# A decoder step on one core: which engine issues the weight loads, the window copies and the stores of new rows

## The chip, the cores and the metric

The kernel runs on one core of one Trainium2 chip. A core has five engines with a queue each: TensorE (PE; its weight loads are listed as PEld), VectorE (DVE), ScalarE (ACT), GpSimd (POOL) and SyncE (SP). Each works through its own list in order and waits on semaphores where it needs another's result. A DMA is an entry of such a list: the engine waits for the conditions of the transfer, issues it, and goes on; the bytes are then moved by 16 DMA engines that all queues share. The metric is the time of one execution in microseconds (us) on the device.

## The reference

One layer of a hybrid decoder, for 256 prompt tokens and for 8 samples of 4 new tokens each over 2048 cached positions. Cut to what is computed:

```python
h = rms_norm(x, norm_g)
c_h, c_b, c_c, c_g, q, n_g, b_g, kv6, m_q, m_g = split_cols(h @ w_in)   # 2048 x 6680
y_a = silu(c_g) * short_conv(c_h, c_b, c_c)                             # group A
o_cmp, o_sel = nsa_cmp_sel(q, rope(q), pos, k_cmp, v_cmp, k_sel, v_sel) # group B, paged cache
o_win = window_attention(rope(q), win_k, win_v)
y_b = silu(n_g) * (g0 * o_cmp + g1 * o_sel + g2 * o_win)
y_m = silu(m_g) * gqa_attend(m_q, mem_k, mem_v)                         # group M, 256 memory tokens
y = rms_norm(x + concat(y_a, y_b, y_m) @ w_out, final_g)
```

`k_cmp` and `v_cmp` are weighted sums over blocks of 64 cached rows, so the whole paged cache is read. Beside `y` the step returns the new K and V rows (`o_kv` in the kernel), the memory K and V of the prompt (`o_mem`), the state of the convolution (`o_conv`), and the window buffers, whose old rows are copied from one place in HBM to another (`o_wk`, `o_wv`).

## The kernel before

**Weights.** All projections are made of 152 weight halves of 128 x 1024 float32 (512 KB): 16 of `w_mem`, 104 of `w_in`, 32 of `w_out`. Half `s` is loaded into `w{s}` (`w_load`, L169; five buffers, tag `wr`), rounded by ACT into `wh` (L179) and subtracted by DVE into `wl` (L184); PE then runs 24 matmuls over it (`product_half`, L198), 16 with `wh` and 8 with `wl`. Inside the matmuls of half `s` the program writes `wh` of half `s+2`, `wl` of half `s+1` and, at matmul 21, the load of half `s+6`. That load may start when `wl` of half `s+1` is done, since it takes that half's buffer. The first four halves are used as they are.

**Cache tiles.** Everything cached comes through six buffers `st` of 128 x 1024 float32 (tag `st`), in the order of a table of due times (`stages`, L644): pages of `ckc` (two DMAs a tile), of `ckk` and `ckv` (four DMAs a tile, `load_pages`, L277, with the page's number read by SP from `ptt` first), and plain tiles of `wk`, `wv`, `mk`, `mv`. A `ckc` tile is multiplied in place, its K half by DVE and its V half by POOL (`cmp_use`, L288; the multiply is L294 on both engines), POOL's half after DVE's, and summed by DVE one tile later (L316). The others go straight into matmuls of PE (`sk` and `od` for pages, `smd` and `omd` for the memory). A new load is issued when a tile is used up (`load_next`, L657).

**What sets the order.** The order on each engine is that of the program text: `chunk` (L114), called after every 12 matmuls, advances the side work by one step. So the loads of weights and of cache tiles stand interleaved in one list, SP's. ACT issues 13 stores: 12 of `o_kv` (L966, L971) and one of `o_conv` (L1059). POOL issues five stores of `o_mem` (L782, L784), beside its 64 multiplies. The 16 window copies (`window_copies`, L625) are issued by SP.

**Completion counters.** A listing of the program's order with its waits shows that the DMAs of SP and ACT together take eight counters in turn (`DMAHW0` to `DMAHW7`), and that each waits for the landing of the one that took the same counter before it, eight DMAs earlier. The DMAs of POOL have eight counters of their own (`DMASW0` to `DMASW7`).

Of the kernel before, what the change touches and what calls it, by code (L numbers as in the profile page):

```python
# [71 lines left out]
def decode_step(ctx, tc, xT, xN, memT, cst, w_in, w_mem, w_out, w_bg, pt, ckc, ckk, ckv, wk, wv, mk, mv,  # L72
# [96 lines left out]
    def w_load(s):  # L169
        if s < NH:  # L170
            raws[s] = pw.tile([128, 1024], F32, name=f"w{s}", tag="wr", bufs=WR)
            if s:
                nc.sync.dma_start(raws[s], wsrc[s])
            loading(DMA_PIECE)

    def w_hi(s):
# [448 lines left out]
    def window_copies():  # L625

        n = 0
        for hf in range(2):
            for rq in range(4):
                for out, in_ in ((o_wk[2 * hf + rq // 2, rq % 2], wk[2 * hf + rq // 2, rq % 2]), (o_wv[hf, rq], wv[hf, rq])):  # L630
                    while now[0] < min(T_WIN[0] + n * T_WIN[1], LAST_PASS):
                        yield 1
                    nc.sync.dma_start(out, in_)
                    n += 1
                    if now[0] >= LAST_PASS:
                        yield T_LAST
# [318 lines left out]
    def kv_tile(part, g, z):  # L955
        if part in (2, 4):
            i = part - 2 + g
            nc.scalar.activation(kk[:, i, :], z, AF.Copy)
            rope_in(i, z)
            if i == 3:  # L960
                yield 1
                yield from rope_out(lambda i, r: nc.scalar.activation(kk[0:32, i, :], r, AF.Copy))
                env["k"] = True
                yield 1
                for i in range(4):
                    nc.scalar.dma_start(o_kv[4 + (i // 2) * 4 + i % 2], kk[:, i, :])  # L966
            return
        dst = zt("A", "kv")
        nc.scalar.activation(dst, z, AF.Copy)
        yield 2  # L970
        nc.scalar.dma_start(o_kv[2 * part + g], dst)  # L971
        if part in (0, 1):
            t = zt("B", "pp")[:, :256].rearrange("p (n j) -> p n j", j=64)
            nc.vector.tensor_tensor(t, dst[:, :256].rearrange("p (n j) -> p n j", j=64),
                                    acmp[:, part].unsqueeze(1).to_broadcast([128, 4, 64]), op=ALU.mult)
            nc.vector.tensor_reduce(pool_p[:, part, g, :], t, axis=AX.X, op=ALU.add)
        if part in (3, 5):
            t = ptr.tile([128, 512], F32, name=f"vtp{part}{g}", tag="t")
            for s in range(2):
                transpose(t[:, s * 128:(s + 1) * 128], dst[:, s * 128:(s + 1) * 128], ident)  # L980
            if part == 3:
                transpose(t[0:64, 256:384], dst[:, 224:288], ident)
            else:
                transpose(t[0:32, 256:384], dst[:, 256:288], ident)
            nc.scalar.activation(vnat[part][:, :, g, :], t[:, :256].rearrange("p (s d) -> p s d", s=2), AF.Copy)
            o = 32 if part == 3 else 0
            nc.scalar.activation(Vn[o:o + 32, g, :], t[o:o + 32, 256:384], AF.Copy)
            env["v", part, g] = True
# [36 lines left out]
    def conv_tile(i, j, z):  # L1025
# [26 lines left out]
        elif j == 2:  # L1052
            nc.vector.tensor_tensor(ct["y"], ct["y"], z, op=ALU.mult)
        else:
            sg = silu2(z)
            yield 1
            nc.vector.scalar_tensor_tensor(mixed[:, i, :], ct["y"], 0.5, sg, op0=ALU.mult, op1=ALU.mult)
            if i == 3:
                nc.scalar.dma_start(o_conv, convo.rearrange("p i t -> p (i t)"))  # L1059
        return  # L1060
        yield

# [408 lines left out]
```

## Time and profile before

| | us |
|---|---|
| median of 3 runs | 649.82 |
| lowest and highest | 647.42, 649.86 |
| the profiled execution, its own time | 649.14 |
| its span, first instruction to last | 647.3 |

The profile lists for each engine the time in which it was busy. Rows of a window give, after the window and its length, each engine's busy time with the number of instructions, then the granted share of the TensorE clock, the mean busy share of the 16 DMA engines, and GB/s. Rows of waits give who waited for whom: total us, times, longest us. Rows of the timeline give start, duration, engine, line, operation, tiles, and in brackets the idle time of the engine before it with what ended it; `SPq` and `ACTq` are those engines' queues, in which DMAs are issued. Names stand without buffer numbers.

### The profile page before, as it was taken

How to read it: one execution, taken by the hardware profiler on the slowest of the kernel's cores; microseconds unless marked ns; L12 is line 12 of the kernel's file. 1: busy time of each engine (PE TensorE's matmuls, PEld its weight loads, DVE VectorE, ACT ScalarE, POOL GpSimd, SP SyncE). 2: the span in 40 equal slices, each digit the busy share in tenths (PEclk: the TensorE clock that was granted, in tenths of full speed). 3: DMA queues.
4: the chain of work that ended last, by engine and by line, in shares of the span. 5: the costliest groups of instructions: out<-in, count | busy, mean ns of one | idle time of the engine just before them, and what ended most of it. 6: DMA issues, size and time to landing. Idle time of an engine off the chain costs nothing.

```text
span 647.3 us, 13704 instructions
## 1 busy us (share of the span) xinstructions
PE 620.8 (96%) x4899; PEld 557.9 (86%) x4899; DVE 453.3 (70%) x721; ACT 290.2 (45%) x517; POOL 81.2 (13%) x79
## 2 busy tenths in 40 slices
PE   9999999999999999999999999999999999999992
PEld 7899999999997898887889787877888889999992
DVE  4788799988675676978669688774764544456754
ACT  4765545435553333543345333443343444445650
POOL 0002333222121210022112121200000000000000
PEclk9999999999999999999999999999999999999996
DMA  8999799989978989977889999898997898488824
GB/s 305 371 420 386 233 316 320 320 287 336 310 265 265 318 310 378 384 256 258 246 270 298 287 303 296 270 304 290 411 363 237 267 274 286 162 273 280 266 76 147
DMA packets 90726, 188.42 MB, mean 291 GB/s; under 512 B 10465, under 2 KB 47202, under 8 KB 90274
## 3 DMA queue, kind: packets, MB, share of 16 engines
q1 hardware_dynamic: 87072, 183.42, 83.5%
q10 hardware_dynamic: 3250, 3.07, 1.4%
q0 software_dynamic: 336, 1.05, 0.4%
q8 instruction: 39, 0.64, 0.4%
q14 instruction: 29, 0.24, 0.1%
HBM read 182.29 MB, written 13.60 MB: 303 GB/s over the span
## 4 chain that ended last, share of the span: by engine, by line
PE 65%; DMA 15%; DVE 12%; issue 3%; SPq 3%; ACT 2%; DVEq 0%; ACTq 0%
PE z L101 51%; DMA st<-ckc 4%; PE od L101 3%; DMA w<-w_in 3%; DVE pooled L316 3%; DMA st<-ckk 2%; DVE wl L184 2%; PE acc L101 2%; PE sk L101 2%; DMA o_kv<-kv 2%; SPq L280 2%; DVE st L294 2%; PE s L101 2%; DMA w<-w_mem 1%; DMA st<-mk 1%
## 5 line engine op out<-in xcount | busy, mean ns | idle before, releaser
L101 PE MATMUL z<-x,wh 128*128 128x288 f32 x1664 | 258.9, 303 | 0.0
L101 PEld LDWEIGHTS z<-x,wh 128*128 128x128 f32 x1664 | 230.0, 188 | 14.6 <-issue 13.0
L184 DVE TENSOR_TENSOR wl<-w,wh 128x1024 fp32r<-128x1024 f32 x148 | 183.5, 1240 | 31.8 <-PE z L101 19.2
L179 ACT ACTIVATE wh<-w 128x1024 fp32r<-128x1024 f32 x148 | 155.0, 1052 | 43.5 <-DMA w<-w_in 28.5
L101 PE MATMUL z<-x,wl 128*128 128x288 f32 x832 | 127.1, 295 | 2.5 <-DVE wl L184 2.3
L101 PEld LDWEIGHTS z<-x,wl 128*128 128x128 f32 x832 | 115.7, 188 | 3.6 <-DVE wl L184 3.6
L294 POOL TENSOR_TENSOR st<-st,cst 128x512 f32<-128x512 f32 x64 | 75.7, 1184 | 299.1 <-DVE st L294 142.6
L316 DVE TENSOR_REDUCE pooled<-st 128x16 f32<-128x1024 f32 x64 | 77.4, 1209 | 2.0 <-POOL st L294 2.0
L294 DVE TENSOR_TENSOR st<-st,cst 128x512 f32<-128x512 f32 x64 | 43.8, 685 | 9.5 <-DMA st<-ckc 8.9
L101 PE MATMUL z<-y,wh 128*128 128x288 f32 x256 | 37.0, 297 | 0.0
L101 PE MATMUL z<-y1a,wh 128*128 128x288 f32 x224 | 35.5, 298 | 0.0
L101 PEld LDWEIGHTS z<-y,wh 128*128 128x128 f32 x256 | 35.1, 188 | 0.0
L101 PEld LDWEIGHTS z<-y1a,wh 128*128 128x128 f32 x224 | 31.6, 188 | 1.6 <-issue 1.6
L1005 DVE SCALAR_TENSOR_TENSOR se<-se,z 128x288 f32<-128x288 f32 x16 | 7.2, 452 | 33.3 <-ACT se L1004 33.3
L101 PE MATMUL sk<-st,qz 128*32 128x256 f32 x320 | 25.8, 385 | 2.7 <-DMA st<-ckk 2.4
L101 PE MATMUL z<-m,wh 128*128 128x256 f32 x192 | 27.0, 286 | 0.7 <-ACT wh L179 0.7
L101 PEld LDWEIGHTS z<-m,wh 128*128 128x128 f32 x192 | 24.6, 191 | 1.4 <-ACT wh L179 0.9
L1164 DVE TENSOR_TENSOR P<-s,cst 128x512 f32<-128x512 f32 x12 | 8.3, 690 | 22.0 <-PE s L101 22.0
L1171 ACT ACTIVATE P<-P,nm 128x128 f32<-128x128 f32 (+1 forms) x32 | 14.2, 445 | 18.2 <-DVE nm L1168 18.2
L378 ACT ACTIVATE S<-sk 128x256 f32<-128x256 f32 x20 | 7.6, 382 | 31.9 <-PE sk L101 31.9
L101 PE MATMUL od<-st,PT 128*32 128x256 f32 x320 | 21.4, 385 | 0.0
L1004 ACT ACTIVATE se<-z 128x288 f32<-128x288 f32 x16 | 6.5, 406 | 31.2 <-PE z L101 31.2
(277 smaller groups left out, 623.6 us busy)
## 6 DMA issues: line engine op xcount, KB each, us to landing
w<-w_in SPq DMA_DIRECT2D x104, 512.0 KB, 6.2
st<-ckc SPq DMA_DIRECT2D x128, 256.0 KB, 5.2
st<-ckk SPq DMA_DIRECT2D x128, 128.0 KB, 4.5
st<-ckv SPq DMA_DIRECT2D x128, 128.0 KB, 3.6
w<-w_out SPq DMA_DIRECT2D x32, 512.0 KB, 5.1
w<-w_mem SPq DMA_DIRECT2D x15, 512.0 KB, 9.1
o_wk<-wk SPq DMA_DIRECT2D x8, 512.0 KB, 6.9
o_wv<-wv SPq DMA_DIRECT2D x8, 512.0 KB, 6.3
```

Of the source, the lines that this page charges most:

```text
L101: nc.tensor.matmul(out, a, b, **kw)
L179: nc.scalar.activation(his[s], raws[s], AF.Copy)
L184: (eng or nc.vector).tensor_tensor(los[s], raws.pop(s), his[s].bitcast(F32), op=ALU.subtract)
L280: nc.sync.dma_start(t[:, i * w:(i + 1) * w], src[ds(v, 1)].rearrange("a p c -> p (a c)"))
L294: done.append(eng.tensor_tensor(tm[:, :, kv], tm[:, :, kv], acmp[:, kv].unsqueeze(1).unsqueeze(1).to_broadcast([128, 2, 4, 64]), op=ALU.mu ...
L316: nc.vector.tensor_reduce(pv.rearrange("p a (c n) -> p c a n", n=2), t.rearrange("p (c a n j) -> p c a n j", c=2, a=4, j=64), axis=AX.X, o ...
L378: nc.scalar.activation(env["S", hf][:, o:o + 256], s[:, :256], AF.Copy)
L1004: nc.scalar.activation(e, z, AF.Tanh, scale=0.5)
L1005: nc.vector.scalar_tensor_tensor(e, e, 1.0, z, op0=ALU.add, op1=ALU.mult)
L1164: nc.vector.tensor_tensor(P[:, h0:h0 + per, :], s.rearrange("p (h s) -> p h s", h=per), causal[:, 256 - L:256].unsqueeze(1).to_broadcast([ ...
L1171: nc.scalar.activation(P[:, h, :], P[:, h, :], AF.Exp, scale=SCALE, bias=nm[:, h:h + 1], accum_out=sm[:, h:h + 1])
```

## The change

Three kinds of DMA move to POOL's list: weight halves 5 to 151, the 16 window copies, and the 13 stores that ACT issued. SP keeps the first five weight halves, the loads of the start, and all cache tiles; the last stores of `o_y` stay with SP and ACT. No computation, buffer or size is changed.

```diff
@@ w_load
             if s:
-                nc.sync.dma_start(raws[s], wsrc[s])
+                (nc.gpsimd if s >= WR else nc.sync).dma_start(raws[s], wsrc[s])
@@ window_copies
-                    nc.sync.dma_start(out, in_)
+                    nc.gpsimd.dma_start(out, in_)
@@ kv_tile
                 for i in range(4):
-                    nc.scalar.dma_start(o_kv[4 + (i // 2) * 4 + i % 2], kk[:, i, :])
+                    nc.gpsimd.dma_start(o_kv[4 + (i // 2) * 4 + i % 2], kk[:, i, :])
...
-        nc.scalar.dma_start(o_kv[2 * part + g], dst)
+        nc.gpsimd.dma_start(o_kv[2 * part + g], dst)
@@ conv_tile
-                nc.scalar.dma_start(o_conv, convo.rearrange("p i t -> p (i t)"))
+                nc.gpsimd.dma_start(o_conv, convo.rearrange("p i t -> p (i t)"))
```

`WR` is 5. The order on PE and DVE is the same as before, and ACT's differs by the 13 stores alone.

The first place is the stretch in which the new K and V rows are made. On SP before, from weight half 56 to half 58 (`w56` is that half, `st49` and `st50` are cache tiles, the brackets name what an entry waits for):

```order
L173 DMA w56_2667<-w_in 128x1024 [waits DMAHW1_49,DVE_49]
L280 DMA st49_2675<-ckk 128x256 [waits DMAHW2_49,DVE_49]
L280 DMA st49_2675<-ckk 128x256 [waits DMAHW3_49]
L280 DMA st49_2675<-ckk 128x256 [waits DMAHW4_49]
L280 DMA st49_2675<-ckk 128x256 [waits DMAHW6_49]
L173 DMA w57_2718<-w_in 128x1024 [waits DMAHW7_49,DVE_49]
L280 DMA st50_2730<-ckc 128x512 [waits DMAHW0_49,DVE_49]
L280 DMA st50_2730<-ckc 128x512 [waits DMAHW1_49]
L173 DMA w58_2785<-w_in 128x1024 [waits DMAHW2_49,DVE_49]
```

On SP in the changed kernel the same tiles stand without the weights between them:

```order
L280 DMA st49_2675<-ckk 128x256 [waits DMAHW5_49,DVE_49]
L280 DMA st49_2675<-ckk 128x256 [waits DMAHW6_49]
L280 DMA st49_2675<-ckk 128x256 [waits DMAHW7_49]
L280 DMA st49_2675<-ckk 128x256 [waits DMAHW0_49]
L280 DMA st50_2730<-ckc 128x512 [waits DMAHW1_49,DVE_49]
L280 DMA st50_2730<-ckc 128x512 [waits DMAHW2_49]
```

The counters now turn among cache tiles alone; the skipped one in the first listing (`DMAHW5`) had gone to a store of ACT.

On ACT before, in the same place, the stores stand behind the rounding of the weights (`wh53`, `wh54`):

```order
L179 ACTIVATE wh53_2689<-w53_2484 128x1024 [waits DMAHW7_49,DVE_49,PE_49]
L969 ACTIVATE kv_2723<-z50_2600 128x288 [waits DMAHW4_49,PE_49]
L334 ACTIVATE Vc_101<-vc0_2725 128x256 [waits PE_49]
L179 ACTIVATE wh54_2739<-w54_2540 128x1024 [waits DMAHW4_49,DVE_49]
L971 DMA o_kv<-kv_2723 128x288 [waits DMAHW0_49,Activation_49]
```

In the changed kernel the last row is gone from ACT and stands on POOL.

On POOL before there are in this place only its multiplies of cache tiles:

```order
L294 TENSOR_TENSOR st43_2449<-st43_2449,cst_93 128x2x256 [waits DMAHW3_49,DMAHW5_49,DMAHW2_49,DMAHW6_49,DVE_49,PE_49]
L294 TENSOR_TENSOR st44_2457<-st44_2457,cst_93 128x2x256 [waits DMAHW5_49,DMAHW6_49,DVE_49,Pool_49]
L294 TENSOR_TENSOR st47_2627<-st47_2627,cst_93 128x2x256 [waits DMAHW3_49,DMAHW1_49,DMAHW4_49,DMAHW0_49,DMAHW7_49,DVE_49,PE_49]
```

On POOL in the changed kernel:

```order
L173 DMA w55_2593<-w_in 128x1024 [waits DMASW6_49,DVE_49]
L294 TENSOR_TENSOR st43_2449<-st43_2449,cst_93 128x2x256 [waits DMAHW4_49,DMAHW5_49,DMAHW3_49,DMAHW6_49,DVE_49,PE_49]
L971 DMA o_kv<-kv_2598 128x288 [waits DMASW7_49,Activation_49]
L173 DMA w56_2667<-w_in 128x1024 [waits DMASW0_49]
L294 TENSOR_TENSOR st44_2457<-st44_2457,cst_93 128x2x256 [waits DMAHW5_49,DMAHW6_49,DVE_49,Pool_49]
L173 DMA w57_2718<-w_in 128x1024 [waits DMASW1_49,DVE_49]
L971 DMA o_kv<-kv_2723 128x288 [waits DMASW2_49,Activation_49]
L173 DMA w58_2785<-w_in 128x1024 [waits DMASW3_49,DVE_49]
```

Each weight half now stands behind a multiply that waits for DVE and for the pages of its tile, and every second one behind a store that waits for ACT.

The second place is the stretch from 80 to 140 us, in which cache tiles of kind `ckc` follow each other. On POOL in the changed kernel:

```order
L173 DMA w27_1058<-w_in 128x1024 [waits DMASW6_49,DMASW4_49,DVE_49]
L294 TENSOR_TENSOR st6_842<-st6_842,cst_93 128x2x256 [waits DMAHW1_49,DMAHW2_49,DVE_49,Pool_49]
L173 DMA w28_1105<-w_in 128x1024 [waits DMASW0_49,DVE_49,Activation_49]
L294 TENSOR_TENSOR st7_890<-st7_890,cst_93 128x2x256 [waits DMAHW3_49,DMAHW4_49,DVE_49,Pool_49]
L173 DMA w29_1146<-w_in 128x1024 [waits DMASW1_49,DVE_49]
```

Here loads and multiplies alternate one to one; before, the multiplies stood alone.

## Rows read from the trace of the kernel before

**Rows 1.** The page's first part: busy us (share of the span) and instructions.

```profile
PE 620.8 (96%) x4899; PEld 557.9 (86%) x4899; DVE 453.3 (70%) x721; ACT 290.2 (45%) x517; POOL 81.2 (13%) x79
```

**Rows 2.** Windows of the stretches (columns as told above).

```profile
20.00:40.00 20.00, 18.32 (x140) 17.19 (x139) 15.16 (x28) 14.08 (x25) 0.93 (x1) 1.00 1.03 378
...
80.00:140.00 60.00, 58.45 (x444) 57.23 (x443) 58.55 (x89) 28.73 (x48) 18.69 (x18) 1.00 0.92 316
...
178.00:262.00 84.00, 80.52 (x687) 71.48 (x685) 58.18 (x88) 33.10 (x56) 12.94 (x11) 1.00 0.89 311
262.00:380.00 118.00, 114.58 (x891) 96.51 (x892) 90.63 (x153) 49.00 (x103) 20.19 (x17) 1.00 0.87 283
380.00:440.00 60.00, 58.39 (x441) 49.33 (x439) 48.28 (x72) 25.14 (x53) 10.30 (x9) 1.00 0.91 293
```

**Rows 3.** Waits of PE from 20 to 40 us: total us, times, longest.

```profile
PE z L101 <- ACT wh L179: 0.7, 1, 0.7
PE z L101 <- DVE wl L184: 0.5, 2, 0.3
```

**Rows 4.** Waits of PE from 178 to 262 us.

```profile
PE sk L101 <- DMA st<-ckk: 1.1, 2, 0.7
...
PE z L101 <- DVE wl L184: 0.8, 2, 0.5
PE kcT L101 <- DVE pooled L316: 0.7, 1, 0.7
```

**Rows 5.** Waits of PE from 380 to 440 us.

```profile
PE sk L101 <- DMA st<-ckk: 1.3, 2, 1.0
```

**Rows 6.** Waits of SP's queue from 178 to 262 us.

```profile
SPq L401 <- DMA o_kv<-kv: 10.2, 2, 7.5
SPq L280 <- DMA o_kv<-kv: 8.1, 3, 3.9
SPq L173 <- DMA o_kv<-kv: 4.8, 2, 2.4
SPq L280 <- DMA o_kv<-qk: 3.5, 1, 3.5
```

**Rows 7.** Waits of all engines from 178 to 262 us: ACT's row for weights.

```profile
ACT wh L179 <- DMA w<-w_in: 28.2, 11, 5.0
```

**Rows 8.** Timeline of DVE: `wl` of weight half 51, which frees the buffer of half 56.

```profile
192.83 1.23 DVE L184 TENSOR_TENSOR wl<-w,wh 128x1024 fp32r<-128x1024 f32 x1 [0.73 <-ACT wh L179]
```

**Rows 9.** Timeline of SP's queue: the issue of weight half 56.

```profile
209.03 0.37 SPq L173 DMA_DIRECT2D w<-w_in  x1
```

**Rows 10.** Timeline of ACT: `wh` of half 56, and the store queued behind it.

```profile
213.31 1.06 ACT L179 ACTIVATE wh<-w 128x1024 fp32r<-128x1024 f32 x1 [2.25 <-DMA w<-w_in]
213.37 0.34 ACTq L971 DMA_DIRECT2D o_kv<-kv  x1
```

**Rows 11.** Timeline of SP's queue at 415 us, with no wait between entries.

```profile
415.75 2.38 SPq L280 DMA_DIRECT2D st<-ckk  x4
418.24 0.37 SPq L173 DMA_DIRECT2D w<-w_in  x1
```

**Rows 12.** The instructions of L784: duration ns min/median/max; then their landing.

```profile
L784 POOL DMA_DIRECT2D o_mem<-mvt x4: 540/543/581, 47.3 to 69.5; - x4
...
DMA to landing us min/median/max: 3.3/5.1/6.0
```

**Rows 13.** Timeline of POOL: the store of L782, four blocks of 128 rows.

```profile
38.72 0.93 POOL L782 DMA_DIRECT2D o_mem<-mixed  x1 [36.88 <-DVE mixed L906]
```

**Rows 14.** The instructions of L173: landing of the weight loads.

```profile
DMA to landing us min/median/max: 3.5/6.0/11.8
```

**Rows 15.** The page's groups of POOL's and DVE's multiplies: busy us, mean ns, idle before.

```profile
L294 POOL TENSOR_TENSOR st<-st,cst 128x512 f32<-128x512 f32 x64 | 75.7, 1184 | 299.1 <-DVE st L294 142.6
L316 DVE TENSOR_REDUCE pooled<-st 128x16 f32<-128x1024 f32 x64 | 77.4, 1209 | 2.0 <-POOL st L294 2.0
L294 DVE TENSOR_TENSOR st<-st,cst 128x512 f32<-128x512 f32 x64 | 43.8, 685 | 9.5 <-DMA st<-ckc 8.9
```

**Rows 16.** Timeline of all engines: DVE's `wl` beside a DMA of POOL.

```profile
47.30 0.55 POOL L784 DMA_DIRECT2D o_mem<-mvt  x1 [7.66 <-DVE mvt L906]
...
47.87 1.22 DVE L184 TENSOR_TENSOR wl<-w,wh 128x1024 fp32r<-128x1024 f32 x1
```

**Rows 17.** Timeline of all engines: `wl` beside a multiply of POOL.

```profile
115.43 1.09 POOL L294 TENSOR_TENSOR st<-st,cst 128x512 f32<-128x512 f32 x1 [2.17 <-DVE st L294]
116.00 1.60 DVE L184 TENSOR_TENSOR wl<-w,wh 128x1024 fp32r<-128x1024 f32 x1
```

## The prediction, made before the result was known

> **What bounds the kernel now.** I read the page's busy times first, then the windows by stretch, then the waits of PE, and last the queues that issue loads. PE is busy for 620.8 of 647.3 us [rows 1], so 26.5 us of idle time are all that better loading could give, and most of it isn't loading: the last stretch works on the norm of the output, which no load feeds. Of the body the windows leave idle 1.68 us (20 to 40), 1.55 (80 to 140), 3.48 (178 to 262), 3.42 (262 to 380) and 1.61 (380 to 440) [rows 2]. From 80 to 140 us DVE is the fuller engine, 58.55 of 60 us [rows 2].
>
> The waits of PE tell which idle time hangs on a load. From 20 to 40 us PE waits 0.7 us for `wh` and 0.5 us for `wl` [rows 3]. From 178 to 262 us it waits 1.1 us for pages, 0.8 us for `wl` and 0.7 us for the sums of cached pages [rows 4]. From 380 to 440 us it waits 1.3 us for pages [rows 5]. Together 5.1 us.
>
> Why loads are late in the middle: SP stands still for 10.2 + 8.1 + 4.8 + 3.5 = 26.6 us from 178 to 262 us until stores of `o_kv` have landed [rows 6]. Those stores are ACT's, but take completion counters of the same eight. Weight loads stand in SP's list behind these waits: half 56 could take its buffer at 192.83 + 1.23 = 194.06 us [rows 8] and is issued at 209.03 [rows 9], 15 us late. ACT then waits for it and starts `wh` at 213.31 after 2.25 us of idling; the next store is queued behind that `wh` and goes out at 213.37 [rows 10], and SP waits for its landing. It is a loop: weight, `wh`, store, SP, weight. ACT idles 28.2 us for weights in this stretch [rows 7], but PE has one or two halves in hand and loses only the 2.6 us above.
>
> **The change part by part.**
>
> *Weight loads to POOL.* 147 issues leave SP. At 0.37 us each [rows 9] that is 54 us of SP's time, none of it on the path by itself. What counts is when a load is issued. On POOL, half 56 waits for its buffer, for POOL's own counters, for one multiply ahead and one store ahead. I walked POOL's new list with the times of before (each entry starts at the later of its release and the end of the one ahead of it). Half 56 comes out 12 us earlier than 209.03, and no half more than 2.4 us later than now; so ACT's 28.2 us of waiting mostly go, and with them PE's 0.8 us on `wl`.
>
> What POOL pays: the trace has no load issued by POOL. The nearest rows are its stores: 0.54 to 0.58 us for 128 rows [rows 12], 0.93 us for four blocks of 128 rows [rows 13]. A weight half has 128 rows, longer ones. I take 0.55 and keep 0.93 as the other end. All 176 moved issues (147 + 16 + 13) then take 97 to 164 us. POOL is busy 81.2 us now [rows 1], so 178 to 245 of 647: it isn't full. Landing: 3.3 to 6.0 us from POOL's issue for 128 KB [rows 12], 3.5 to 11.8 us for weights from SP [rows 14]. I take the same median landing, 6.0 us, and keep 3.3 and 11.8 as ends: shorter, since a weight then shares the DMA engines with the pages queued on SP and no longer stands behind all of them; at the other end 5.8 us longer, still less than the 12 us by which half 56 is issued sooner.
>
> *What is queued behind POOL's new waits.* A multiply of a cache tile now stands behind a weight issue. From 80 to 140 us both alternate. The buffer is freed when `wl` ends, and DVE's own multiply of 685 ns follows it before POOL's may start [rows 15]; an issue of 0.55 us fits into that. Cost nothing. At 0.93 us it would push POOL's multiply by 0.25 us, of which the price is in the second rival. The sum of the tile is taken one tile later and has that time in hand.
>
> *Window copies to POOL.* 16 issues, source and target in HBM. POOL's issue of such a copy is shown by no row; 0.55 to 0.93 us by the same rows. Behind one of them stands a weight half, with 3 us and more between two halves. Cost nothing.
>
> *Stores of new rows to POOL.* ACT loses 13 issues, SP loses the 26.6 us of standing still, and its page loads of that stretch go out that much sooner. This is what pays PE's 1.1 us on pages and 0.7 us on sums. A store on POOL waits for ACT's copy; the weight half behind it waits with it, for the copy and no longer for the landing.
>
> *SP at 380 to 440 us.* SP issues without a gap there: four pages in 2.38 us, then a weight at once [rows 11]. Without the weights a tile's pages go out 0.37 us sooner for each half between. That covers the longest wait of 1.0 us [rows 5]. I take 1.0 of the 1.3 us.
>
> *The start.* From 20 to 40 us the DMA engines' share is 1.03 [rows 2]; there is no rate to spare, and a weight that lands sooner takes it from the tokens that PE needs next. I take half of the 1.2 us, 0.6, with ends of 0 and 1.2 (a loss of as much can't be left out).
>
> A rule speaks against gaining more. Rows first: the DMA engines' share is 0.89 from 178 to 262 us, so 0.11 x 84 = 9 us of them are unused there, and 1.03 in the start [rows 2]. The Trainium skill, "DMA: Bandwidth & Descriptors", section "Issuing engines are not separate DMA queues", says that DMAs of all engines run on the same 16 engines, and that issuing from several only saves the issuer's time. By that rule the start gives 0 and the sum below is 0.6 us smaller. The gain of the middle is issue time and waiting in a list, and would stand.
>
> Sum: 2.6 (178 to 262) + 1.0 (380 to 440) + 0.6 (start) = 4.2 us. Softmax chains and the tail stay. The profiled execution took 649.14 us, 0.7 below the median of 649.82; 649.1 - 4.2 = 644.9, and I say **645**.
>
> **The rivals.**
>
> *The gain is given back by the pages (no change).* Weights that land sooner take the DMA engines from pages that PE and DVE wait for; DVE already waits 8.9 us for pages of `ckc` [rows 15]. For it: shares of 0.87 to 0.92 in all stretches of the body [rows 2]. Against it: the 9 us unused, and SP's pages go out sooner as well. It would leave some 1 us of the 4.2: 648. The case in which POOL's list couples weights to ACT and DVE as SP's did ends at the same time.
>
> *POOL's multiplies run into DVE's subtractions (slower).* Place: 80 to 140 us, where DVE has 1.45 us left of 60. A multiply of POOL lies now beside DVE's sum, 1209 ns against 1184 [rows 15]. Where it lies beside `wl`, `wl` takes 1.60 us [rows 17] in place of 1.22 [rows 16]. If weight issues push all 18 multiplies of the stretch [rows 2] over `wl`, DVE pays up to 18 x 0.38 = 6.8 us, all on the path. From 178 on the gain of 3.6 remains: 649.1 - 3.6 + 6.8 = 652. It decides from an issue of over 0.69 us on, the time of DVE's multiply. The Trainium skill, "SBUF — State Buffer", section "Who interferes with whom", has this rule: a DVE instruction with two inputs from SBUF contends with a GpSimd instruction that reads SBUF. The trace agrees for the multiply, 1.60 against 1.22 us. For a DMA's issue it shows no such price: `wl` takes 1.22 us beside one [rows 16].
>
> *More than forecast.* If sooner loads also pull in the softmax chains, half of the 11.7 us idle in the body goes: 643 to 639.
>
> **How the numbers follow.** Forecast and more than forecast 0.55, the pages rival 0.30, the slower rival 0.10, and 0.05 for another loss of POOL's issue (each longer than 0.93 us, or landing later than ACT has in hand). A measurement of this kernel can tell about 0.5%, 3.2 us. Faster by over that: below 646.6, 0.55; within it 0.30; slower 0.15. The range runs from 639 to 652: it takes in the second rival's 652 and leaves out both ends beyond, 2 in 10. The forecast's own range is 642 to 647.
>
> **What the profile after would show.** SP's waits for `o_kv` gone, and ACT's 28.2 us for weights from 178 to 262 us down to a few. POOL's DMAs of 128 rows at about 0.55 us and POOL at about 180 us busy. PE idle under 1.5 us from 178 to 262 us, DVE at 80 to 140 us unchanged. The prediction is wrong if POOL's issues take over 0.7 us, if weights from POOL land later than from SP, or if PE's waits for `sk` grow.

## The result, and the profile after

The changed kernel took 642.92 us (median of 4 runs, 642.56 to 643.56), the kernel before 649.81 us beside it (4 runs, 647.42 to 649.86). The ratio is 0.9904, with a 95% interval of 0.9876 to 0.9931: 1% faster, 6.9 us. In two later series, on two different chips, the same kernel came out at 643.99 us against 648.08 (0.9934, 0.9904 to 0.9964) and 644.05 against 649.75 (0.9909, 0.9876 to 0.9941). The time lies inside the forecast's own range of 642 to 647.

The page of the profile after begins so (busy us, share of the span, instructions; then the DMA queues with packets, MB and their share of the 16 engines' span):

```profile
span 640.9 us, 13712 instructions
...
PE 615.6 (96%) x4899; PEld 556.1 (87%) x4899; DVE 455.5 (71%) x721; ACT 289.6 (45%) x517; POOL 177.0 (28%) x255
...
q1 hardware_dynamic: 65392, 97.96, 44.4%
q0 software_dynamic: 22624, 88.33, 40.1%
```

Beside [rows 1], POOL's busy time rose from 81.2 to 177.0 us, and PE's fell from 620.8 to 615.6. The same 4899 matmuls were busy 5.2 us less. That is the first hint that "busy" isn't all work here, since the work of both kernels on PE is the same.

The windows of the stretches, with the columns of [rows 2]:

```profile
20.00:40.00 20.00, 17.38 (x133) 16.24 (x132) 14.95 (x28) 14.50 (x25) 4.05 (x8) 1.00 1.02 382
80.00:140.00 60.00, 57.83 (x435) 56.16 (x434) 59.79 (x87) 28.11 (x47) 28.86 (x35) 1.00 0.92 314
178.00:262.00 84.00, 82.67 (x722) 75.60 (x721) 65.02 (x98) 36.89 (x62) 33.41 (x48) 1.00 0.93 332
262.00:380.00 118.00, 114.83 (x893) 96.76 (x892) 87.43 (x148) 46.00 (x99) 33.18 (x41) 1.00 0.87 286
380.00:440.00 60.00, 59.91 (x465) 50.58 (x464) 47.81 (x74) 27.10 (x57) 17.63 (x22) 1.00 0.90 302
```

Read the counts of matmuls in brackets: from 178 to 262 us PE does 722 of them where it did 687, from 380 to 440 us 465 for 441, but from 80 to 140 us 435 for 444, with DVE at 59.79 of 60 us. Two stretches gained and one lost.

Since the counts shift with the windows, I measured each stretch by its matmuls. Both kernels issue the same 4899 in the same order, so the matmul that starts at 178 us before can be found in the trace after, and the difference of the two starts tells how far PE is behind or ahead there. After minus before, in us: +0.7 at 80 us, +1.8 at 140 and 178, -2.9 at 262 and 380, -6.8 at 460, -6.7 at the end. By stretch that is +0.7 for the start (up to 80 us), +1.1 (80 to 140), -4.8 (178 to 262), 0.0 (262 to 380) and -3.9 (380 to 460). All stretches below are read in this way.

SP no longer stands still for the landing of `o_kv` [rows 6]. What its queue waits for from 178 to 262 us (total us, times, longest) is now that cache tiles are used up:

```profile
SPq L546 <- DVE pooled L316: 12.8, 2, 10.5
SPq L401 <- PE sk L101: 6.5, 1, 6.5
SPq L280 <- DVE pooled L316: 6.3, 4, 2.9
SPq L401 <- DVE pooled L316: 6.0, 2, 3.1
```

ACT's 28.2 us of waiting for weights [rows 7] are gone from its list of waits; it has a new wait, for the landing of an earlier store of a `kv` tile, now POOL's, and PE's waits of that stretch [rows 4] have shrunk to two:

```profile
ACT kv L969 <- DMA o_kv<-kv: 6.5, 1, 6.5
...
PE vtp L105 <- ACT kv L969: 0.7, 1, 0.7
PE kcT L101 <- DVE pooled L316: 0.6, 1, 0.6
```

From 380 to 440 us [rows 5] PE has no wait of 0.3 us or more left. At the start [rows 3] it waits 2.3 us for `wh` in place of 0.7.

**Lateness that is counted as busy.** PE's idle time from 178 to 262 us fell by some 2 us only (3.48 before, 1.33 after), but PE gained 4.8 us. Most of the rest is in the matmuls on pages. Here is PE's timeline (start us, us, then the instruction, and the idle time before it) around the tile of `sk` at 204 us, first before, then after:

```profile
204.25 0.62 PE L101 MATMUL sk<-st,qz 128*32 128x256 f32 x4
205.53 1.67 PE L101 MATMUL sk<-st,qz 128*32 128x256 f32 x12 [0.66 <-DMA st<-ckk]
207.13 0.40 PE L101 MATMUL z<-x,wh 128*128 128x288 f32 x1
```

```profile
206.78 1.07 PE L101 MATMUL sk<-st,qz 128*32 128x256 f32 x16
207.78 0.40 PE L101 MATMUL z<-x,wh 128*128 128x288 f32 x1
```

A tile has 16 matmuls of 32 columns on four pages. When all four pages are there, the tile takes 1.07 us: the starts lie in fours, within 0.02 us of each other, and the next four follow 0.22 us later. When the pages come one by one, the matmuls of the last page to come start alone, 0.22 us apart, and the tile took 205.53 + 1.67 - 204.25 = 2.95 us: 1.88 us lost, of which the list of waits shows 0.66. The tile at 428 us shows the same, 431.77 - 428.21 = 3.56 us in place of 1.07, with 0.37 + 0.95 us of it as waits:

```profile
428.21 0.63 PE L101 MATMUL sk<-st,qz 128*32 128x256 f32 x4
429.20 0.59 PE L101 MATMUL sk<-st,qz 128*32 128x256 f32 x2 [0.37 <-DMA st<-ckk]
430.75 1.02 PE L101 MATMUL sk<-st,qz 128*32 128x256 f32 x10 [0.95 <-DMA st<-ckk]
```

Taken from the first to the last start of a tile (0.69 us when the pages are there), five tiles of the kernel before were late: 2.58 and 1.68 us (at 204 and 215 us), 1.41, 1.62 and 3.19 us (at 389, 409 and 428 us). The excess is 2.9 us in the first stretch and 4.1 us in the second. After the change all 20 tiles take 0.69 to 0.7 us. So pages of `sk` account for 2.9 of the 4.8 us of the first stretch, and for all of the 3.9 us of the second. The other 1.9 us of the first, again by the starts of the same matmuls: 1.65 us on three halves whose `wl` came late before (at 253, 257 and 262 us) and 1.04 us on `imp`, less 0.77 us on the new wait of `vtp`. Before, `imp` waited for DVE, which had itself stood 3.67 us for a page of `ckc` at 209 us.

### The profile page after: what moved, and what is told of

Same layout as the page of the kernel before. It is cut to its first block, busy times and chain, and to the rows that moved or that the text cites. A ratio compares the mean times of both kernels' runs of the same rounds, so it can differ in the third digit from the quotient of the medians.

```text
span 640.9 us, 13712 instructions
## 1 busy us (share of the span) xinstructions
PE 615.6 (96%) x4899; PEld 556.1 (87%) x4899; DVE 455.5 (71%) x721; ACT 289.6 (45%) x517; POOL 177.0 (28%) x255
## 4 chain that ended last, share of the span: by engine, by line
PE 75%; DVE 10%; DMA 8%; issue 3%; ACT 1%; SPq 1%; POOL 0%; DVEq 0%; ACTq 0%; POOLq 0%
PE z L101 59%; PE od L101 3%; DVE pooled L316 3%; PE sk L101 3%; DMA xn<-xN 3%; PE acc L101 2%; DVE wl L184 2%; DVE st L294 2%; DMA st<-ckc 2%; PE s L101 2%; DMA st<-ckv 1%; DMA w<-w_mem 1%; PE pt L105 1%; DMA o_kv<-kv 1%; SPq L280 1%
## 5 line engine op out<-in xcount | busy, mean ns | idle before, releaser
L101 PEld LDWEIGHTS z<-x,wh 128*128 128x128 f32 x1664 | 229.8, 188 | 14.6 <-issue 12.8
L184 DVE TENSOR_TENSOR wl<-w,wh 128x1024 fp32r<-128x1024 f32 x148 | 187.8, 1270 | 35.6 <-PE z L101 17.5
L173 POOL DMA_DIRECT2D w<-w_in x104 | 59.2, 569 | 159.8 <-DVE wl L184 71.8
L173 POOL DMA_DIRECT2D w<-w_out x32 | 17.1, 533 | 97.4 <-DVE wl L184 57.8
```

What stands on the lines that cost most here:

```text
L101: nc.tensor.matmul(out, a, b, **kw)
L173: (nc.gpsimd if s >= WR else nc.sync).dma_start(raws[s], wsrc[s])
L184: (eng or nc.vector).tensor_tensor(los[s], raws.pop(s), his[s].bitcast(F32), op=ALU.subtract)
```

## The experiments

Four theories stood against each other. A: SP's standing still for the landing of ACT's stores held up the loads; the stores are the part that pays. B: weights in SP's list are the cause. C: POOL's issue pushes its multiply onto `wl` from 80 to 140 us, and that is the 1.1 us lost. D: the start's +0.7 us is a price of POOL too, or else chance. Parts of the change were run alone, in pairs, and with one thing altered.

**The stores alone.** The kernel before with this edit (and the same for the other store of `o_kv` and for `o_conv`):

```diff
-        nc.scalar.dma_start(o_kv[2 * part + g], dst)
+        nc.gpsimd.dma_start(o_kv[2 * part + g], dst)
```

> The kernel before, with only the 13 stores of ACT (o_kv, o_conv) issued by POOL; weights and window copies stay on SP. Theory A (the middle gain comes from breaking the loop weight, wh, store, SP): SP no longer stands still for landings of o_kv (26.6 us before), ACT's wait for weights from 178 to 262 us falls from 28.2 to under 10 us, and most of the 4.8 us that PE gained between 181 and 262 us appears here too: 645.5 us, 4 below the kernel before; nothing changes at the start, from 80 to 140 us or from 380 to 440 us. Rival B (what counts is that weights leave SP's list; the stores alone matter little): PE from 178 to 262 us stays within 1 us of before, 649 us. If A and B each hold half, 647.

Measured: 643.27 us against 649.84, ratio 0.9900 (0.9865 to 0.9935). By stretch: -5.1 us from 178 to 262, 0.0 from 80 to 140, -0.3 from 380 to 460. SP's queue has no wait for `o_kv` left, and ACT none for weights. In the middle all tiles of `sk` take 0.69 us, but around 404, 423 and 444 us three still take 2.06, 1.57 and 1.18. The gain is larger than theory A's (645.5 us), and as large as that of the whole change, though not by the same stretches: the gain from 380 us on is missing, and so is the loss from 80 to 140. A stands; B falls for the middle.

**The weights alone.** The kernel before with

```diff
-                nc.sync.dma_start(raws[s], wsrc[s])
+                (nc.gpsimd if s >= WR else nc.sync).dma_start(raws[s], wsrc[s])
```

> The kernel before, with only the weight halves from the sixth on issued by POOL; stores stay on ACT and window copies on SP. Theory A: at the start PE is 0.7 us later than before, from 80 to 140 us 1.2 us later (POOL's issue pushes its multiply onto wl), from 380 to 440 us about 3.9 us earlier; from 178 to 262 us SP still stands still for landings of o_kv, some 20 us, but only pages stand behind that, so PE gains 2 to 4 us of the 4.8: in all 644 us. Rival B (weights in SP's list are all of it): the whole gain of the change, 643 us or less. Rival C (without the stores moved nothing is gained in the middle): the stretch from 178 to 262 us as before and 647.5 us.

Measured: 648.69 us against 649.84, ratio 0.9995 (0.9967 to 1.0024), no difference. By stretch: +1.1 from 80 to 140, -0.7 from 178 to 262, +1.6 from 380 to 460. Theory A had 644 us, rival C 647.5: the time is worse than either, and C is nearest. SP's queue from 178 to 262 us (total, times, longest):

```profile
SPq L546 <- DMA o_kv<-kv: 8.7, 2, 5.1
...
SPq L280 <- DMA o_kv<-qk: 5.4, 1, 5.4
...
SPq L401 <- DMA o_kv<-kv: 5.1, 1, 5.1
SPq L280 <- DMA o_kv<-kv: 4.0, 2, 2.9
```

SP still stands still for 8.7 + 5.4 + 5.1 + 4.0 = 23.2 us, now with cache tiles alone behind it, and the tile of `sk` at 205 us is later than ever:

```profile
205.25 0.63 PE L101 MATMUL sk<-st,qz 128*32 128x256 f32 x6
208.63 1.53 PE L101 MATMUL sk<-st,qz 128*32 128x256 f32 x10 [2.75 <-DMA st<-ckk]
```

ACT waits for no weight in this stretch, and PE gains next to nothing net. By what it works on: it gets back the same 1.65 us on `wl` as with the whole change, and 1.04 us on `imp`, for which it now comes later itself. It loses 0.71 us on the tiles of `sk` and 1.28 us on the matmuls behind the late one: after 2.75 us without work the granted clock was 0.50, the lower of TensorE's two levels (1.2 GHz), from 209.0 to 212.4 us:

```profile
209.10:212.40 3.30, 3.30 (x15) 2.48 (x11) 1.24 (x3) 1.60 (x4) 0.44 (x1) 0.50 0.50 138
```

So late weights did cost PE time, 1.65 us, which either part alone gives back; the larger part was pages queued behind SP's waits, and only moving the stores gives that back. From 380 to 460 us it is similar: SP waits 5.2 us for the landing of `o_conv`, and two tiles of `sk`, at 420 and 437 us, take 2.01 and 3.22 us, although no weight stands in SP's list. Behind the second the clock was 0.50 again, from 441.1 to 444.5 us, and the matmuls that follow took 1.7 us longer than before; without that the stretch would be about even, an estimate. Taking the weights off is not enough there; in the kernel with the stores alone, taking the stores off wasn't either. Only where both are gone are the tiles on time (in one later run, one of 20 takes 1.11 us).

**The window copies alone.** The kernel before with

```diff
-                    nc.sync.dma_start(out, in_)
+                    nc.gpsimd.dma_start(out, in_)
```

> The kernel before, with only the 16 window copies issued by POOL. Theory: they stand on no path; SP still stands still for landings of o_kv and the tiles of sk at 204, 215, 409 and 428 us still take more than 0.69 us: within 1 us of the kernel before, 649.8 us. Rival: the copies, when they leave SP, free pages behind them: 647.5 us or less.

Measured: 662.41 us against 648.08, ratio 1.0221 (1.0151 to 1.0290): 2% slower, which neither expected. By stretch: -1.9 from 178 to 262, +14.6 from 380 to 460. POOL's timeline tells why:

```profile
434.73 0.54 POOL L633 DMA_DIRECT2D o_wk<-wk  x1
435.27 0.49 POOL L633 DMA_DIRECT2D o_wv<-wv  x1
...
438.13 0.49 POOL L633 DMA_DIRECT2D o_wv<-wv  x1
440.50 0.49 POOL L633 DMA_DIRECT2D o_wk<-wk  x1 [1.88 <-DMA o_wk<-wk]
442.32 0.49 POOL L633 DMA_DIRECT2D o_wv<-wv  x1 [1.33 <-DMA o_wv<-wv]
```

After its last multiply POOL's list holds nothing but the ten copies left, and nothing makes the first eight wait; the last two wait, 1.88 and 1.33 us, until the copy eight places earlier has landed. So 10 x 512 KB go out within some 8 us. Landing of the pages issued from 425 to 445 us (min, median, max), and the windows of that time:

```profile
DMA to landing us min/median/max: 3.3/5.2/18.8
```

```profile
435.00:445.00 10.00, 6.25 (x41) 3.46 (x40) 2.45 (x3) 2.03 (x4) 4.59 (x10) 1.00 0.99 367
445.00:455.00 10.00, 0.01 (x1) 0.04 (x2) 0.00 (x0) 0.00 (x0) 0.00 (x0) 0.50 0.98 323
```

The longest landing of these pages was 6.0 us in the kernel before and 6.5 in the changed one, here it is 18.8. PE stands for the ten microseconds from 445 us on, and its granted clock falls to 0.50, where it stays until 458.7 us. Of the 14.6 us lost 13.8 are in the tiles of `sk`. At the 367 GB/s of the first of these windows 5.2 MB take 14.3 us, an estimate of the right size, though other loads share that rate.

**Stores and window copies, without the weights.** Is it the weights in POOL's list that keep the copies apart? The changed kernel with the weights back on SP:

```diff
-                (nc.gpsimd if s >= WR else nc.sync).dma_start(raws[s], wsrc[s])
+                nc.sync.dma_start(raws[s], wsrc[s])
```

> The changed kernel with the weights back on SP: POOL issues only stores and window copies. Theory P (in POOL's list only the weights, which wait for buffers, keep the window copies apart; without them ten copies of 128 KB rows go out within 8 us from about 430 us on and every page behind them lands 8 to 19 us late, as with the windows alone): ten of the copies are issued within 10 us, one tile of sk near 435 us takes over 10 us, and of the gain of the stores 13 us are lost: 656 us. Rival (with the windows alone the loss came from ACT's o_conv, on whose landing SP waited 2.7 us before): with the stores on POOL no such wait is left, and the time is that of the stores alone, 643.3 us, within 1.

Measured: 659.42 us against 649.75, ratio 1.0153 (1.0098 to 1.0208); theory P had 656, the rival 643.3. By stretch: -5.1 from 178 to 262 as with the stores alone, +14.8 from 380 to 460. Ten copies go out between 433.58 and 442.67 us, and the longest landing of a page there is 19.3 us. In place of the one tile of over 10 us that was expected, two are late, of 5.75 us (at 437 us) and 6.93 us (at 454 us). The kind of loss and its size are theory P's, and its rival falls: the copies are harmless on POOL only because weights, which wait for buffers, stand between them. In the changed kernel the first of the ten goes out at 441.62 us and the second at 506.13.

**Stores and weights, without the window copies.** The changed kernel with the copies back on SP:

```diff
-                    nc.gpsimd.dma_start(out, in_)
+                    nc.sync.dma_start(out, in_)
```

> The changed kernel with the window copies back on SP: POOL issues only stores and weights. Theory: the window copies gain nothing; the tiles of sk all take 0.69 us, 178 to 262 us gains 4.8 us and 380 to 445 us 3.9 us as in the changed kernel: within 1 us of the changed kernel on the same chip. Rival (a window copy on SP waits for a completion counter and holds pages up): over 1.5 us slower than the changed kernel on the same chip.

Measured: 643.30 us against 649.75, ratio 0.9890 (0.9856 to 0.9925); the changed kernel beside it took 644.05. By stretch +1.1, -5.4 and -3.4. One tile of `sk`, at 434 us, takes 1.11 us, where all were expected to take 0.69. The copies gain nothing that the time shows, as the theory said.

**Shared counters, or the place in the list?** From 380 to 460 us both stores and weights had to leave SP. The weights of that stretch may hold pages up by their place in SP's list, or because they share completion counters with the pages. The changed kernel with halves 92 to 110 issued by ACT, off SP's list but on the shared counters:

```diff
-                (nc.gpsimd if s >= WR else nc.sync).dma_start(raws[s], wsrc[s])
+                (nc.sync if s < WR else nc.scalar if 92 <= s <= 110 else nc.gpsimd).dma_start(raws[s], wsrc[s])
```

> The changed kernel, but weight halves 92 to 110 (those loaded around 370 to 445 us) are issued by ACT: they are off SP's list, as in the changed kernel, and share completion counters with SP's pages again, as in the kernel before. Theory L (it is the place in SP's list that made pages late there): every tile of sk from 380 to 445 us still takes 0.69 us and PE's 3.9 us are kept, 643 us. Theory C (it is the shared counters: SP waits until a weight that ACT issued has landed): SP waits for landings of weights there, two to four tiles of sk take 1.2 to 3 us again, and 2.5 to 4 us are lost, 646 us. A loss that shows only in wh (ACT waits in its own list for a buffer) would be a third thing and speak for neither.

Measured: 659.60 us, ratio 1.0171 (1.0115 to 1.0227); the changed kernel beside it took 643.99. Theory C is right in kind and far too small: 15.6 us lost. The queue of SP from 365 to 460 us, and PE's tile at 431 us:

```profile
SPq L280 <- DMA w<-w_in: 25.3, 12, 5.6
```

```profile
430.87 0.84 PE L101 MATMUL sk<-st,qz 128*32 128x256 f32 x6
435.32 1.02 PE L101 MATMUL sk<-st,qz 128*32 128x256 f32 x10 [3.61 <-DMA st<-ckk]
```

Twelve times SP waits until a weight of ACT's has landed, 25.3 us in all, though ACT issued it. Three tiles of `sk` (at 412, 431 and 450 us) take 1.74, 5.10 and 6.10 us. Two more things add to it: ACT's `PT` once stood 7.4 us behind a weight that waited for its buffer, and shortly before its end PE waited 3.7 us for `pt`; and the granted clock was 0.50 in three stretches (378.5 to 381.9, 436.5 to 439.9 and 453.5 to 460.4 us). So not all of the 15.6 us are the counters', but the coupling itself is shown: tiles are late with no weight in SP's list. How the 4.1 us of the kernel before divide between counters and place is not shown.

**The 80 to 140 us stretch.** In the changed kernel (DVE and POOL, from the timeline of all engines):

```profile
101.87 1.27 DVE L184 TENSOR_TENSOR wl<-w,wh 128x1024 fp32r<-128x1024 f32 x1
...
103.06 0.68 DVE L294 TENSOR_TENSOR st<-st,cst 128x512 f32<-128x512 f32 x1
...
103.67 1.21 DVE L316 TENSOR_REDUCE pooled<-st 128x16 f32<-128x1024 f32 x1
103.69 0.59 POOL L173 DMA_DIRECT2D w<-w_in  x1 [1.63 <-issue]
104.30 1.10 POOL L294 TENSOR_TENSOR st<-st,cst 128x512 f32<-128x512 f32 x1
...
104.80 1.70 DVE L184 TENSOR_TENSOR wl<-w,wh 128x1024 fp32r<-128x1024 f32 x1
```

The buffer is free when `wl` ends, at 103.14 us. POOL starts its issue 0.55 us later and needs 0.59 us; so its multiply starts at 104.30, though DVE's part was done at 103.74, and runs 0.6 us beside the next `wl`, which takes 1.70 us. Two edits test this. The first leaves the early weights on SP; the second writes each load at the first matmul of the next half, behind the multiply in POOL's list:

```diff
-                (nc.gpsimd if s >= WR else nc.sync).dma_start(raws[s], wsrc[s])
+                (nc.gpsimd if s >= 42 else nc.sync).dma_start(raws[s], wsrc[s])
```

> The changed kernel, but the weight halves up to number 41 are issued by SP as before (POOL issues them from number 42 on). Theory: the start (+0.7 us) and the stretch from 80 to 140 us (+1.2 us) lose only because POOL issues weights there; wl beside POOL's multiply goes back to before's 1.3 us mean from 1.44, and PE reaches 140 us with no shift against the kernel before. The later gains (4.8 us from 178 to 262 us, 3.9 us from 380 to 440 us) stay: 641.0 us, 1.9 below the changed kernel. Rival: the shift of the start is made up later anyway (PE waits for something else in the middle): within 0.5 us of the changed kernel, 642.9.

```diff
-            if s == DIRECT and n == 0:
+            if n == 0:
                 w_load(s + WR)
-            if n == LOAD_AT:
-                w_load(s + WR + 1)
```

> The changed kernel, but each weight load is written at the first matmul of the next half, so that in POOL's list it stands behind the multiply of a cache tile and no longer ahead of it. Theory (POOL's issue of 0.59 us plus its lag behind the release of 0.3 to 0.55 us is more than the 0.685 us of DVE's own multiply, so POOL's multiply slides onto wl): wl from 80 to 140 us no longer takes 1.70 us beside a multiply, and the 1.2 us lost there come back: 641.7 us. Against it, weights are issued about 1 us later each, which the median slack of 7.3 us between landing and wh covers. Rival 1 (the overlap stays, the pair is set by DVE's order and not by POOL's issue): 80 to 140 us as in the changed kernel, 642.9 us. Rival 2 (later loads cost PE waits at the start or in the middle): 644 us or more.

Measured: 641.75 us (ratio 0.9882, 0.9846 to 0.9919) and 641.67 us (0.9885, 0.9849 to 0.9922), both against 649.84. From 80 to 140 us PE loses nothing in either, -0.2 and 0.0 against the kernel before. The groups of `wl` in that window (count, busy us, mean ns) for the kernel before, the changed kernel, then with the early weights on SP, then with the later load:

```profile
L184 DVE TENSOR_TENSOR wl<-w,wh 128x1024 fp32r<-128x1024 f32 x19 | 24.6, 1292 | 0.1
```

```profile
L184 DVE TENSOR_TENSOR wl<-w,wh 128x1024 fp32r<-128x1024 f32 x18 | 25.2, 1402 | 0.1
```

```profile
L184 DVE TENSOR_TENSOR wl<-w,wh 128x1024 fp32r<-128x1024 f32 x19 | 24.2, 1276 | 0.1
```

```profile
L184 DVE TENSOR_TENSOR wl<-w,wh 128x1024 fp32r<-128x1024 f32 x19 | 23.7, 1249 | 0.1
```

In the changed kernel six of these subtractions take 1.70 to 1.71 us; before, two took 1.60 and 1.76. C is shown for this stretch, by two independent edits. The second also reorders some work of PE from 127 us on (up to there its shift is as small, 0.05 us), so of its other stretches nothing is concluded.

The other order of the same two costs POOL and not DVE. In the kernel before, at 63 us, `wl` starts first and takes its usual time, and the multiply takes 2.08 us in place of 1.09:

```profile
63.13 1.23 DVE L184 TENSOR_TENSOR wl<-w,wh 128x1024 fp32r<-128x1024 f32 x1
63.23 2.08 POOL L294 TENSOR_TENSOR st<-st,cst 128x512 f32<-128x512 f32 x1 [0.70 <-ACT wh L179]
```

So it is in all 28 pairs of both traces that overlap by 0.4 us or more: the one that starts second is the longer for it.

**Both edits together** (halves up to 41 on SP, each load at the first matmul):

> The changed kernel with both repairs: weight halves up to 41 issued by SP, and each load written at the first matmul of the next half. Theory: both repair the same loss (POOL's multiplies on wl from 80 to 140 us), so together they give no more than each alone: 641.5 us, within 0.7. Rival: they add up, since the later load also frees the middle (with the late load alone PE had no idle time from 178 to 262 us): 640.3 us or less.

Measured: 646.55 us, ratio 0.9979 (0.9948 to 1.0011), with the changed kernel at 643.99 beside it: a loss of 2.6 us that I hadn't expected. Between 140 and 178 us PE falls 3.2 us back. Half 41, the last on SP, stands there behind pages and is issued at 141.93 us, after the two younger halves that POOL issued at 139.26 and 140.71; ACT waits 5.8 us for it (its longest wait for a weight from 138 to 182 us), and PE 2.8 us for ACT's `Pm` behind that. With the later load alone, in the same order of PE, nothing is lost there (0.0). A load order that two queues share can turn round at the seam. The two edits don't add up.

**The zero, and the start.** The changed kernel itself, twice more:

> The changed kernel unchanged, profiled once more, as a zero for readings by stretch: what differs between its two profiles is chance. Theory: the start varies by 0.5 us or more either way from run to run (the two kernels with weights on SP at the start came out at +0.3 and -0.5 us against the kernel before), so the +0.75 us of its first profile needs no cause; the loss from 80 to 140 us (1.1 us), the gains from 178 to 262 us (4.8 us) and from 380 to 445 us (3.9 us) come again within 0.5 us. Rival: the start is late by 0.75 us again, and is a price of POOL's issue. Time 642.9 us, within 0.5.

> The changed kernel unchanged, as the neighbour of the kernel with weights up to half 41 on SP on one chip. Expected 643 to 644 us; the stretch from 80 to 140 us costs 1.1 us against the kernel before for the fourth time, the start anything between -0.5 and +1.8 us.

Measured: 643.99 us, 0.6 above the margin of what was expected, and 644.05 us, with the ratios given above. By stretch, the three profiles of the changed kernel: +1.1, +1.2, +1.1 us from 80 to 140; -4.8, -5.4, -5.0 from 178 to 262; -3.9, -3.8, -3.8 from 380 to 460. These repeat. The start doesn't: PE's shift at 80 us is +0.7, +1.7 and +2.4 us for this one kernel. Kernels with weights on POOL from the start have -0.1 to +3.8 us there, kernels with weights on SP -0.5 to +2.3. In two of these profiles, with the stores and one other part on POOL, the granted clock was 0.50 for 3.4 us of the start (31.0 to 34.4 and 35.7 to 39.2 us). D stays open: one kernel's spread of 1.7 us is larger than the 0.7 us to be explained, and one profile of the kernel before is the zero for all of them.

**The best version once more**, on the same chip as the changed kernel:

> Weights up to half 41 on SP, the rest on POOL, once more, now on the same chip as the changed kernel. Theory: the stretch from 80 to 140 us gains 1.1 us against the changed kernel, and so does the time: 1.1 us less than the changed kernel beside it, within 0.7. Rival: the 1.2 us between their medians was the difference of two chips, and the two are equal within 0.4 us.

Measured: 641.65 us (6 runs, 639.79 to 642.63), ratio 0.9884 (0.9845 to 0.9922), against 644.05 us (8 runs, 642.31 to 644.72) for the changed kernel: 2.4 us less, where 1.1 were expected. Of the difference 1.3 us are the stretch from 80 to 140 (-0.2 against +1.1); 1.3 us lie in the start, and so may be chance. Over both chips it beat the kernel before by 1.2%.

The stretches of the kernels with parts of the change side by side (PE's shift against the profile of the kernel before, us):

| on POOL | 80 to 140 | 178 to 262 | 380 to 460 | median us, ratio |
|---|---|---|---|---|
| stores | 0.0 | -5.1 | -0.3 | 643.27, 0.9900 |
| weights | +1.1 | -0.7 | +1.6 | 648.69, 0.9995 |
| windows | -0.2 | -1.9 | +14.6 | 662.41, 1.0221 |
| stores, windows | -0.2 | -5.1 | +14.8 | 659.42, 1.0153 |
| stores, weights | +1.1 | -5.4 | -3.4 | 643.30, 0.9890 |
| all three | +1.1 | -4.8 | -3.9 | 642.92, 0.9904 |
| all, weights from 42 on | -0.2 | -4.8 | -3.9 | 641.75, 0.9882 |

## Why the prediction was right, and where it wasn't

**The time.** 645 was said, 642.9 measured, faster as forecast. The sum was 4.2 us of gain, the profile shows 6.7 net: 8.7 gained in two stretches, 1.1 lost in one, 0.7 lost in a start that no run pins down, and 0.2 over the rest. That the sum came so near is in part luck: the two gains were put 5.1 us too low, and 2.4 us of that were made up for by a loss put at nothing and a start that was to gain 0.6. At 642.9 it touches the third rival (643 to 639), but not by its mechanism: the softmax chains of 262 to 380 us gained nothing.

**The middle, 2.6 us said, 4.8 measured.** The link was right: SP's waits for landings of `o_kv` and the 28.2 us of ACT are gone, and the walk of POOL's list came true: half 56 went out at 198.59 us, 10.4 us sooner (12 said), and no half more than 2.6 us later (2.4 said). Of the split one half was right, that the stores pay the pages. The other half, that `wl` needs the weights moved, was not: with the stores alone the same 1.65 us come back, since the loop is broken at that end too. With the weights alone it is broken as well, but SP still stands for 23.2 us, the pages stay late, and PE gains 0.7 us net, for 5.1 with the stores. The sizes of the terms were too small. Pages: I took 1.1 us from the list of waits, and the two tiles lost 2.9, because matmuls on pages that come one by one are counted as busy. `wl`: 0.8 said, 1.65 measured. The 0.7 us of `kcT <- pooled` that I counted in is still there, at 0.6, and 0.7 us of `vtp <- kv` have come in new; the wait for `imp` of 0.8 us, which I left out as part of the softmax, went away with the late page of `ckc` ahead of it.

**380 to 440 us, 1.0 us said, 3.9 measured.** The step that failed is the price of the 1.3 us of waits: the tiles' lateness was 4.1 us. The reason given, weights in SP's list at 0.37 us each, is only a part of it. Without the weights but with ACT's `o_conv`, SP stands 5.2 us for that store's landing and two tiles are 3.9 us late together, nearly as before. That store stood in no term of the prediction.

**The weights' issue on POOL, "fits into the 685 ns".** The issue was sized rightly: 0.55 us said, 527 to 591 ns at the median.

```profile
L173 POOL DMA_DIRECT2D w<-w_in x104: 527/591/983, 46.4 to 488.0; - x104
L173 POOL DMA_DIRECT2D w<-w_out x32: 527/527/554, 495.9 to 606.0; - x32
...
DMA to landing us min/median/max: 3.8/6.4/10.7
```

But I let it start when the buffer came free; POOL starts 0.3 to 0.55 us after that (0.55 in the row above), so 0.55 + 0.59 us stand against 0.685. The second rival had the place, the mechanism and the price of one overlap; its point of decision, an issue over 0.69 us, should have been the delay and the issue together. It came true in part, 1.1 us of its 6.8, since only six multiplies of the stretch were still running when a `wl` started. The weights land at a median of 6.4 us from POOL, for 6.0 from SP [rows 14]: that is one of the signs named for being wrong, but it is 0.4 us, and ACT waits for no weight in the middle. The Trainium skill, "SBUF — State Buffer", section "Who interferes with whom", has a DVE instruction with two inputs from SBUF contend with a GpSimd instruction that reads SBUF, and the trace agrees: `wl` takes 1.70 us beside POOL's multiply and goes back to a mean of 1276 ns where the multiply isn't pushed.

That a DMA's issue has no such price holds, but [rows 16] don't show it: there `wl` starts at 47.87 us, and the issue has ended at 47.85. Another place of the kernel before does, and in the changed kernel 16 subtractions that lie beside an issue for 0.35 us or more, and beside no multiply, take 1.21 to 1.23 us:

```profile
59.36 1.22 DVE L184 TENSOR_TENSOR wl<-w,wh 128x1024 fp32r<-128x1024 f32 x1
59.74 0.54 POOL L784 DMA_DIRECT2D o_mem<-mvt  x1 [4.80 <-DMA st<-ckc]
```

**The window copies, "cost nothing".** True of the whole change, and for the reason that stood beside it in passing: a weight half stands behind each copy. I used that to show that a copy doesn't delay the weights. It works the other way: the weights delay the copies. Without them the copies cost 14.6 us, which is the first rival's mechanism (transfers that take the DMA engines from pages) at over four times its price (14.6 us for 3.2). The Trainium skill, "DMA: Bandwidth & Descriptors", section "Issuing engines are not separate DMA queues", says that DMAs run on the same 16 engines whichever engine started them; the runs agree, with pages landing after up to 18.8 us behind copies that another engine issued. Its second sentence, that issuing from more engines saves only the issuer's time, is narrower than what the runs show: the stores alone, 13 issues, brought 6.6 us, and what they saved was above all SP's waiting for their landing.

**The start, 0.6 us of gain said.** What of it came can't be told: PE was 0.7 to 2.4 us late there in the three profiles of the changed kernel, no gain in any, and they spread by 1.7 us.

**What was said of the profile after**: POOL at about 180 us (177.0), SP's and ACT's waits gone, PE idle under 1.5 us from 178 to 262 (1.33), all right; DVE from 80 to 140 us unchanged, wrong (59.79 for 58.55).

## What to carry to other kernels

When several queues share completion counters, look for a fast queue that waits for the landing of another's slow store: moving a handful of stores to a queue with counters of its own can be worth more than moving all the loads. Price late operands by the length of the whole group of matmuls against one that is on time, since in this kernel the lateness of small matmuls that lost their neighbours was counted as busy. And before moving DMAs that depend on nothing, ask what makes them wait now: on a list where nothing does, they go out at once and can hold up the loads behind them, as ten copies did here.

## What the runs showed of the hardware

- A tile of 16 matmuls of 32 columns on four pages takes 1.07 us with the pages there and 2.95 to 3.56 us when they come one by one, of which 0.66 to 1.32 us are listed as waits.
- POOL starts a load's issue 0.29 to 0.55 us after the `wl` that it waits for has ended, where SP took 0.03 to 0.06 us in the kernel before; the issue takes 527 to 591 ns on POOL (medians by tensor), and 370 ns on SP for the weights of `w_in` [rows 9].
- SP waits for the landing of a DMA that ACT issued: 26.6 us for `o_kv` before [rows 6], 25.3 us for 19 weights on ACT.
- Ten copies of 512 KB within HBM, issued in a row, raised the longest landing of a page from 6.0 to 18.8 us.
- A subtraction of DVE that starts while POOL's multiply runs takes 1.59 to 2.10 us in place of 1.22; one that starts first keeps its 1.22 us, and the multiply takes 1.58 to 2.13 us in place of 1.09 (28 pairs, kernel before and changed kernel).
- With PE without work from 445 to 455 us the granted clock was 0.50, the lower of its two levels (1.2 GHz), and with the weights alone on POOL it was 0.50 from 209.0 to 212.4 us, after a wait of 2.75 us.
